# A second-level split for product 4 in the first superblock, and product 2's stored sums made one superblock later

## The chip, the cores and the metric

One core of one Trainium2 chip runs the kernel. The metric is device time in microseconds (us). Three runs of the kernel before took 1461.13, 1463.53 and 1457.79 us, so its median is 1461.13 us. One more execution was taken by the hardware profiler; all rows of the profile come from it, and their times count from the start of its span. TensorE, which multiplies, is called PE; VectorE is DVE, ScalarE is ACT, GpSimd is POOL, and SP is the queue of SyncE, which only starts transfers.

## The reference

```python
x: (8, 1024, 1024)   w1: (1024, 4096)   w2: (4096, 1024)   float32

h = x @ w1
h = 0.5 * h * (1 + np.tanh(np.sqrt(2 / np.pi) * (h + 0.044715 * h ** 3)))
return (h @ w2).astype(np.float32)
```

Two matrix products with a GELU between them. The kernel computes in fp16 with float32 accumulation.

## The kernel before

**Blocks and products.** The 8192 rows of x are worked off in eight superblocks of 1024 rows. In each, both matmuls are done by Winograd's form of Strassen's method: the operands are cut into 2 x 2 blocks ("11", "12", "21", "22"), sums and differences of blocks are formed, and seven products of half size take the place of eight. The products are numbered 1 to 7. Products 1, 2 and 3 use a weight block as it is, products 5, 6, 7 and 4 use sums of weight blocks (`SUMS` is 5, 6, 7, 4).

**Second level.** A product can be cut once more in the same way, which the class `Inner` does: seven small products of 16 matmuls on 256 columns each (L1129), in place of 64 matmuls on 512 columns (L1184). For that it needs the split of the weight operand: the four small sums 5, 6, 7 and 4 of it, which `split_jobs` makes, and the four small differences of the other operand, which `Inner.make` makes.

**Superblocks 0 and 1** are the first to see the weights. `matmul1` makes the first matmul in eight pairs of columns (j = 0 to 7), and `matmul2_made` the second. In them the sums of W2 are made (`make`, L890 stores them in superblock 1), and the splits of every W2 operand, too. The splits go to HBM, into `in_d[m]`, so that superblocks 2 to 7 (`matmul1_late`, `matmul2`) can run all seven products of the second matmul on the second level. Which products run on the second level in superblocks 0 and 1 is set by `deep`: product 3 in superblock 0, product 4 in superblock 1.

**The order around the change.** The second matmul of superblocks 0 and 1 runs its products in the order 1, 2, 5, 6, 3, 7, 4. A plain product has four steps, one for each 128 rows (q = 0 to 3); a product on the second level has seven (n = 1 to 7), in the order 1, 5, 6, 2, 7, 3, 4 of its small products. After each step, `run` works off the jobs that the table `FILL[sb]` has for it, written by hand. "36:p25" means: after step 6 of product 3, make small sum 5 of product 2's split. The letters are

- `g`: the sums of the GELU's output, which lie in pool "gcp" or over their operands;
- `w53`: piece 3 of W2's sum 5; sum 6 is made over block 11, sum 7 over block 12, sum 4 over block 21;
- `p25`: small sum 5 of product 2's split, with its store (L1012 from POOL's queue, L166 from SP's);
- `a45`: small difference 5 of product 4's other operand;
- `t`: the transposes of one block of the next x (SP's queue, in superblock 0);
- `x5`, `q5`, `i2`: sums of the next x, sums of W1's quad 0, and the small sums of one operand of the next first matmul.

DVE works these jobs off in program order, together with the additions that bring a product out of PSUM (`post`). In superblock 1 all sixteen transposes of the next x are issued together, in the program after step 0 of product 5.

**Queues.** `load_in_order` issues on SP's queue and keeps the program's order there. An entry whose data or buffer isn't ready holds up what stands behind it. `nc.gpsimd.dma_start` issues on POOL's queue. Before, product 2's and 3's splits are stored through SP, all others through POOL.

**Buffers.** Pool "up" has 24 buffers of 4 KB per partition (`unit`, `half`). In the second matmul of superblocks 0 and 1 the W2 pieces hold 16 of them (four for each block, or for the sum made over it), sum 5 another 4, the four blocks of the next x 4; the splits, W1's quad 0 for the next superblock and the result rows of a product on the second level want the rest. A store's buffer comes free when the store has landed. Pool "mp" has two buffers, which hold small sums 7 and 4.

**The first matmul of superblock 1** loads W1's quad 0 back (four loads issued through SP after step 0 of product 7), makes its sums 5, 6, 7, 4 on DVE and then, for the later superblocks, small sums of its operands 7 and 3 (pair j = 0) and 1 and 5 (pair j = 2), as `FIRST_INNER` says; those of operand 2 are `i2` in the table. Each is four additions of 128 x 512.

Of the kernel before, what the change touches and what calls it, by code (L numbers as in the profile page):

```python
# [9 lines left out]
DT = mybir.dt.float16  # L10
# [4 lines left out]
P = 128  # L15
# [8 lines left out]
SUMS = tuple(W_SUM)  # L24
# [13 lines left out]
""".split()  # L38
BEGIN = {"m37": (0,), "m24": (1,2), "m34": (3, 4)}
SPLIT_IN_M1 = ()  # L40
FIRST_INNER = {0: (7, 3), 2: (1, 5)}


def slots(table):
    return {(int(k[0]), int(k[1])): v.split() for k, v in (row.split(":") for row in table.split(";"))}
# [4 lines left out]
    ;20:g50 w50 w51;21:g51 w52;22:w53 g52;23:g53 p14  # L50
    ;50:w60 w61;51:w62 w63;52:g30 g31;53:g32 g33
    ;60:p35 p36 t0;61:a35 p37 t1;62:a37 p34 t2;63:t3 a36
    ;31:w70;32:a33;33:w71;34:w72;35:w73;36:p25;37:p26
    ;70:p27 p24;71:w40 w41;72:w42 w43;73:x5;40:x7;41:x6;42:x3 q5 q6 q7 q4
    ;43:i2""".replace("\n    ", "")),
    slots("""10:g60 w50;11:g61 w51;12:g62 w52;13:g63 w53
    ;20:g50 p55;21:g51 p56;22:g52 p57;23:g53 p54
    ;50:w60 w61;51:w62 w63;52:g30 g31;53:g32 g33
    ;60:p65 w70;61:p66 w71;62:p67 w72;63:p64 w73
    ;30:p75 w40;31:p76 w41;32:p77 w42;33:p74 w43  # L60
    ;70:p45 x5;71:p46 a45;72:x7 p47;73:a47 a46
    ;42:p44;43:a43;44:x6;45:x3;46:i2;47:i3""".replace("\n    ", "")),
)


# [11 lines left out]
def kernel(  # L77
# [7 lines left out]
    nc = tc.nc  # L85
# [10 lines left out]
    NI = I // P // 2  # L96
    OH = O // 2
# [10 lines left out]
    mp = ctx.enter_context(tc.tile_pool(name="mp", bufs=2))  # L108
# [15 lines left out]
    in_d = {m: dram.tile([P, 4, NI // 2, OH // 2], DT, name=f"in_d{m}") for m in range(1, 8)}  # L124
# [7 lines left out]
    def psum():  # L132
        return pp.tile([P, HT], F32, name="ps")
# [4 lines left out]
    def unit(rows, cols):  # L138
        return up.tile([P, rows, cols], DT, name="u")
# [396 lines left out]
    def matmul1(xs, sb, quads, start=None):  # L536
# [26 lines left out]
        for j in range(NI // 2):  # L563
# [60 lines left out]
            for job in jobs[:half]:  # L624
                job()
            for m in FIRST_INNER.get(j, ()) if sb == 1 else ():
                quads[0].inner_sums(m)
# [222 lines left out]
    def matmul2_made(sb, g, keep_w1, xb):  # L850
# [24 lines left out]
        def keep(b):  # L875
            if sb == 0:
                for q in range(NI // QC):
                    load_in_order(w2_at(q, term.get(b, b)), raw[b][q])
# [13 lines left out]
        def pieces(m):  # L892
            return raw[W_TERM[m]] if m in W_TERM else sums[m]

        def rows(t, q):
            return t[:, :, q * P:(q + 1) * P]

        s2, a, p5, t6, at = {}, {}, {}, {}, {}
        operands = {1: "11", 2: "12", 4: "22", 7: "21", 5: "11", 3: "12"}
        parts = {m: {} for m in (1, 2, 3, *SUMS)}  # L900
        splits = {m: split_jobs(m, lambda m=m: pieces(m), parts[m]) for m in parts}
        deep = {m: Inner(m, g[operands[m]]) for m in ((3,), (4,))[sb]}
        for m, d in deep.items():
            d.base, d.y = [], parts[m]
            d.rows = lambda r, t, o={3: "12", 4: "21"}[m], q=load_in_order if m == 3 else nc.gpsimd.dma_start: store_rows(sb, o, r, t, q)
# [1 line left out]
        def run(key):  # L907
            for job in FILL[sb].get(key, ()):
                kind, m, n = job[0], int(job[1]), int(job[2:] or 0)
                if kind == "g" and m == 6:  # L910
                    s2[n] = gcp.tile([P, NI, P], GT, name="gc")
                    tt(s2[n], rows(g["22"], n), rows(g["21"], n), SUB, True)
                elif kind == "g" and m == 5:
                    tt(rows(g["11"], n), s2[n], rows(g["11"], n), ADD, True)
                elif kind == "g":
                    tt(rows(g["12"], n), rows(g["12"], n), s2[n], SUB, True)
                elif kind == "w":
                    make(m, n)
                elif kind == "p":
                    splits[m][SUMS.index(n)]()  # L920
                elif kind == "a":
                    deep[m].make(n)
                elif kind == "t":
                    x_transpose(xb, load_in_order, xs.blocks, (m,))
                elif kind == "x":
                    xs.make(m, pin=True)
                elif kind == "q":
                    quad.sum(m, pin=True)
                elif kind == "i" and sb:
                    xs.make_inner(m)  # L930
                elif kind == "i":
                    quad.inner_sums(m)

        def post(m, q, bank):
            after = deep.get({6: 3, 7: 4}.get(m))
            if after:
                if q % 2 == 0:
                    after.base.append(half())
                so_far = after.base[q // 2][:, q % 2, :]
            if after and m == 6:  # L940
                tt(so_far, p5[q], bank, ADD, True)
            elif m in (1, 5, 6):
                t = {1: a, 5: p5, 6: t6}[m]
                t[q] = temp()
                act_copy(t[q], bank)
            elif m == 4:
                c = temp()
                act_copy(c, bank)
                store(sb, "21", q, c)
            else:  # L950
                t = {2: a, 3: t6, 7: p5}[m][q]
                tt(t, t, bank, ADD, True)
                at[q] = store(sb, {2: "11", 3: "12", 7: "22"}[m], q, t)
            if after and m == 7:
                act_copy(so_far, bank)
# [8 lines left out]
        for m, name, first in (  # L964
            (1, "a", True), (2, "b", True), (5, "c", True), (6, "a", False),
            (3, "c", False), (7, "a", False), (4, "a", False),
        ):
            if m in deep:
                deep[m].pieces = pieces(m)
                for n in deep[m].steps(deep[m].base):  # L970
                    if (m, n) == (4, 1):
                        quad = StoredHalf(0)
                    run((m, n))
                continue
            for q in range(NQ):
                if first:
                    banks[name].append(psum())
                bank = banks[name][q]
                matmuls2(bank, s2[q] if m == 6 else rows(g[operands[m]], q), pieces(m), first)
                post(m, q, bank)  # L980
                if (m, q) == (5, 0) and sb == 0:
                    xb = x_cast(sb + 1, nc.gpsimd.tensor_copy(out=pace, in_=p5[0][:, :2]))
                if (m, q) == (5, 3):
                    keep("22")
                if (m, q) == ((5, 0) if sb else (6, 0)):
                    xs = XOps(x_transpose(xb, load_in_order, which=range(4 if sb else 0)))
                if (m, q) == (7, 0) and sb == 0:
                    quad = MadeQuad(0, False, True)
                if (m, q) == (1, NQ - 1) and sb == 0:
                    sums[5] = [unit(2, HALF) for _ in range(NI // QC)]  # L990
                    for t in sums[5]:
                        act_copy(t[:, 0, :1], warm)
                    bring("22", act_copy, True)
                    keep("21")
                    keep("12")
                run((m, q))
        return xs, [quad]

    def split_jobs(m, pieces, t):

        def operand(v, h):
            if isinstance(v, int):
                return t[v][:, h * QC:(h + 1) * QC, :]
            k, b = int(v[0]) - 1, int(v[1]) - 1
            return chunks(pieces()[2 * k + h])[:, b]

        def make(n):
            u, op, v = W_SUM[n]
            t[n] = (mp.tile([P, NI // 2, OH // 2], DT, name="mu") if n in (7, 4) and m != 4 else unit(NI // 2, OH // 2))
            for h in range(2):  # L1010
                tt(t[n][:, h * QC:(h + 1) * QC, :], operand(u, h), operand(v, h), op, True)
            (load_in_order if m in (2, 3) else nc.gpsimd.dma_start)(out=in_d[m][:, SUMS.index(n)], in_=t[n])  # L1012

        return [lambda n=n: make(n) for n in SUMS]

# [166 lines left out]
    def matmuls2(bank, a, pieces, first):  # L1182
        for c in range(NI):
            tc.keep_in_program_order(nc.tensor.matmul(  # L1184
                pair(bank),
                lhsT=a[:, c, :],
                rhs=chunks(pieces[c // QC])[:, :, c % QC, :],
                start=(first and c == 0),
                stop=(c == NI - 1),
                skip_group_check=not first,  # L1190
            ))
# [93 lines left out]
    for sb in range(NSB):  # L1285
        if sb < 2:
            g, nxt = matmul1(xs, sb, quads, first if sb == 0 else None)
            xs, quads = matmul2_made(sb, g, None if sb else quads[-1].keep_raw, nxt)
            continue
        g, early, nxt = matmul1_late(xs, sb, quads, g_late or g_tiles())  # L1290
# [32 lines left out]
```

## Time and profile before

| | us |
|---|---|
| median of three runs | 1461.13 |
| lowest and highest of them | 1457.79, 1463.53 |
| the profiled execution's own time | 1460.05 |
| its span | 1458.30 |

| stage of the profiled execution | from, to (us) |
|---|---|
| superblock 0, first matmul | 0, 112.7 |
| superblock 0, products 1, 2, 5, 6 | 112.7, 168.0 |
| superblock 0, product 3 (second level) | 168.0, 180.2 |
| superblock 0, product 7, product 4 | 180.2, 194.1, 208.0 |
| superblock 1, first matmul | 209.3, 309.3 |
| superblock 1, products 1, 2, 5 | 309.3, 323.2, 337.0, 350.8 |
| superblock 1, products 6, 3, 7 | 350.8, 364.6, 378.4, 392.2 |
| superblock 1, product 4 (second level) | 392.2, 404.5 |
| superblocks 2 to 7, some 175 us each | 404.5, 1458.3 |

How to read the rows: a row of an engine's order of time gives the start, the duration, the engine and line, the operation, the tile written and read, the number of instructions merged into it, and in brackets the idle time ahead of it and what ended that. Rows of the stages give for each engine its busy time and its count, then the clock that TensorE was granted, the mean busy share of the 16 DMA engines, and what they moved. A row of the waits gives who waited for whom, the total, how often, and the longest. The granted clock is 1.00 in all stages. The page names L142 for nearly all of DVE's work, since one helper records it; which job a row is follows from its place in the tables and from its shape: two instructions of 128 x 1024 are one `p` job, one of 128 x 2048 is a `w`, `a`, `x` or `q` job.

### The profile page before, as it was taken

How to read it: one execution, taken by the hardware profiler on the slowest of the kernel's cores; microseconds unless marked ns; L12 is line 12 of the kernel's file. 1: busy time of each engine (PE TensorE's matmuls, PEld its weight loads, DVE VectorE, ACT ScalarE, POOL GpSimd, SP SyncE). 2: the span in 40 equal slices, each digit the busy share in tenths (PEclk: the TensorE clock that was granted, in tenths of full speed). 3: DMA queues.
4: the chain of work that ended last, by engine and by line, in shares of the span. 5: the costliest groups of instructions: out<-in, count | busy, mean ns of one | idle time of the engine just before them, and what ended most of it. 6: DMA issues, size and time to landing. Idle time of an engine off the chain costs nothing.

```text
span 1458.3 us, 28912 instructions
## 1 busy us (share of the span) xinstructions
PE 1447.5 (99%) x10731; PEld 1048.6 (72%) x10731; DVE 1210.6 (83%) x2019; ACT 711.6 (49%) x1460; POOL 583.1 (40%) x596
## 2 busy tenths in 40 slices
PE   9999999999999999999999999999999999999998
PEld 5444644444577888778877788777887778877887
DVE  5657859758788889888898898988989889888887
ACT  5665115641168621785128841488225872168621
POOL 1442113213369401792028820498005960068400
PEclk9999999999999999999999999999999999999999
DMA  9999999898799999999999999999999999986594
GB/s 329 339 334 381 320 279 368 303 302 260 276 387 249 289 373 367 340 231 337 356 359 311 240 364 347 365 283 234 384 352 364 253 265 371 358 338 230 203 409 168
DMA packets 199372, 460.13 MB, mean 316 GB/s; under 512 B 75200, under 2 KB 80320, under 8 KB 198336
## 3 DMA queue, kind: packets, MB, share of 16 engines
q1 hardware_dynamic: 179328, 378.59, 75.9%
q0 software_dynamic: 19904, 79.70, 17.1%
q8 instruction: 84, 1.38, 0.4%
q14 instruction: 56, 0.46, 0.1%
HBM read 370.15 MB, written 102.76 MB: 324 GB/s over the span
## 4 chain that ended last, share of the span: by engine, by line
PE 85%; DMA 8%; issue 4%; POOL 1%; DVE 1%; ACT 0%; SPq 0%; POOLq 0%; DVEq 0%
PE ps L1129 36%; PE ps L719 23%; PE ps L502 19%; PE ps L1184 6%; DMA gc<-in_w_dram 3%; DMA u<-in_w_dram 2%; DMA w_d<-u 1%; PE ps L435 1%; POOL u L172 1%; DMA xb<-in_x_dram 1%; DVE u L142 0%; PE ps L412 0%; SPq L166 0%; ACT u L169 0%; DMA u<-in_x_dram 0%
## 5 line engine op out<-in xcount | busy, mean ns | idle before, releaser
L169 ACT COPY tmp<-ps 128x512 f32<-128x512 f32 (+1 forms) x528 | 263.6, 539 | 231.1 <-PE ps L502 146.5
L502 PE MATMUL ps<-u 128*128 128x512 f16 x1472 | 343.8, 379 | 4.4 <-DVE tmp L142 1.9
L1129 PE MATMUL ps<-u,gc 128*128 128x256 f16 x2704 | 308.7, 273 | 0.0
L1129 PEld LDWEIGHTS <-gc 128*128 128x128 f16 x2816 | 275.5, 98 | 32.1 <-DMA u<-in_d 0.2
L142 DVE TENSOR_TENSOR tmp<-tmp,ps 128x256 f32<-128x256 f32 (+1 forms) x368 | 197.2, 544 | 72.7 <-PE ps L719 31.0
L142 DVE TENSOR_TENSOR u<-u 128x2048 f16<-128x2048 f16 (+3 forms) x292 | 223.4, 808 | 33.6 <-PE ps L1129 14.1
L502 PEld LDWEIGHTS <-u 128*128 128x128 f16 x1472 | 143.8, 98 | 146.8 <-issue 3.0
L719 PEld LDWEIGHTS <-u 128*128 128x128 f16 x2096 | 205.1, 98 | 57.2
L1129 PE MATMUL ps<-u,g 128*128 128x256 f16 x2000 | 234.8, 273 | 0.0
L848 POOL DMA_DIRECT2D out_dram<-u x48 | 35.2, 733 | 491.4 <-DVE u L142 433.4
L1129 PEld LDWEIGHTS <-g 128*128 128x128 f16 x2112 | 206.6, 98 | 24.4
L719 PE MATMUL ps<-u 128*128 128x256 f16 x1372 | 221.0, 273 | 0.0
L169 ACT COPY ps<-ps 128x256 f32<-128x256 f32 (+1 forms) x208 | 95.2, 458 | 219.3 <-PE ps L1129 219.3
L515 ACT ACTIVATE g<-tmp 128x512 f16<-128x512 f32 x282 | 173.9, 639 | 57.5 <-DVE tmp L142 56.6
L142 DVE TENSOR_TENSOR ps<-tmp,ps 128x256 f32<-128x256 f32 x444 | 181.3, 426 | 17.1 <-PE ps L719 9.4
L169 ACT COPY u<-ps 128x512 f32<-128x512 f32 (+1 forms) x114 | 66.3, 587 | 179.9 <-PE ps L1129 146.2
L142 DVE TENSOR_TENSOR u<-u,ps 128x512 f32<-128x512 f32 x174 | 118.4, 684 | 40.1 <-PE ps L1129 19.3
L515 ACT ACTIVATE g<-ps 128x512 f16<-128x512 f32 x230 | 137.9, 600 | 25.3 <-PE ps L719 15.3
L1184 PE MATMUL ps<-u,g 128*128 128x512 f16 x640 | 138.8, 379 | 0.0
L771 POOL TENSOR_TENSOR tmp<-tmp 128x512 f32<-128x512 f32 x96 | 122.0, 1273 | 40.6 <-DVE tmp L142 30.5
L142 DVE TENSOR_TENSOR tmp<-ps,tmp 128x512 f32<-128x512 f32 x126 | 86.7, 690 | 49.0 <-PE ps L502 41.6
L1184 PEld LDWEIGHTS <-g 128*128 128x128 f16 x640 | 62.6, 98 | 75.3
(72 smaller groups left out, 1570.7 us busy)
## 6 DMA issues: line engine op xcount, KB each, us to landing
u<-w_d SPq DMA_DIRECT2D x347, 512.0 KB, 9.3
u<-in_d SPq DMA_DIRECT2D x162, 512.0 KB, 9.7
gc<-in_w_dram SPq DMA_DIRECT2D x48, 512.0 KB, 5.9
out_dram<-u POOLq DMA_DIRECT2D x48, 512.0 KB, 7.4
g<-w_d SPq DMA_DIRECT2D x45, 512.0 KB, 8.2
w_d<-u POOLq DMA_DIRECT2D x40, 512.0 KB, 6.8
w_d<-u SPq DMA_DIRECT2D x32, 512.0 KB, 10.0
xb<-in_x_dram POOLq DMA_DIRECT2D x56, 256.0 KB, 6.9
```

What stands on the lines that cost most here:

```text
L142: i = nc.vector.tensor_tensor(out=out, in0=in0, in1=in1, op=op)
L169: tc.keep_in_program_order(nc.scalar.copy(out=out, in_=in_))
L172: pool_last[0] = nc.gpsimd.tensor_copy(out=out, in_=in_)
L435: tc.keep_in_program_order(nc.tensor.matmul(bank[:, cols], lhsT=w[:, k, :], rhs=self.xs.blocks[f"{a}{r}"][:, k, cols], start=r == 1 and k ...
L502: tc.keep_in_program_order(nc.tensor.matmul(bank, lhsT=w, rhs=x, start=first and k == 0, stop=k == n - 1, skip_group_check=not first,))
L515: gelu_last[0] = nc.scalar.activation(out=out, in_=src, func=GELU, scale=scale)
L719: tc.keep_in_program_order(nc.tensor.matmul(out, lhsT=w, rhs=x, start=first and k == 0, stop=k == 1, skip_group_check=not first,))
L771: tc.keep_in_program_order(nc.gpsimd.tensor_tensor(out=t, in0=t, in1=temp("p", m), op=ADD))
L848: return start(out=rows, in_=src)
L1129: tc.keep_in_program_order(nc.tensor.matmul(bank[:, i * OH // 2:(i + 1) * OH // 2], lhsT=t[:, c, i * P:(i + 1) * P], rhs=self.weights(j, c ...
L1184: tc.keep_in_program_order(nc.tensor.matmul(pair(bank), lhsT=a[:, c, :], rhs=chunks(pieces[c // QC])[:, :, c % QC, :], start=(first and c ...
```

## The change

Four things are changed.

1. In superblock 0 product 4 runs on the second level too (`deep` has 3 and 4). Its split is made there from sum 4, and not stored (`keep` is false): superblock 1 makes and stores it, as before. w40 to w43 are made earlier, since the split needs all of sum 4; x5, x7, x6, x3 and the sums of W1's quad 0 move into the steps of product 4.
2. Product 2's split (p25, p26, p27, p24) is made and stored in superblock 1, in the steps of product 6, instead of superblock 0. All four of its small sums take buffers of pool "up".
3. The splits of products 5 and 6 in superblock 1 are stored through SP's queue instead of POOL's, as is product 2's.
4. Operand 2's small sums of W1's quad 0 move from the table into pair 0 of superblock 1's first matmul; operand 3's go to pair 2, operand 1's to pair 4, operand 5's to pair 6. In superblock 1, x5 and x7 are made some steps later.

```diff
-FIRST_INNER = {0: (7, 3), 2: (1, 5)}
+FIRST_INNER = {0: (2, 7), 2: (3,), 4: (1,), 6: (5,)}
...
 FILL = (
...
-    ;31:w70;32:a33;33:w71;34:w72;35:w73;36:p25;37:p26
-    ;70:p27 p24;71:w40 w41;72:w42 w43;73:x5;40:x7;41:x6;42:x3 q5 q6 q7 q4
-    ;43:i2
+    ;31:w70;32:a33;33:w71;34:w72;35:w73;36:w40;37:w41 w42
+    ;70:w43 p45;71:p46 a45;72:p47 a47;73:a46;41:p44;42:a43;43:x5;44:x7;46:x6;47:q5 x3 q6 q7 q4
...
-    ;60:p65 w70;61:p66 w71;62:p67 w72;63:p64 w73
+    ;60:p65 w70 p25;61:p66 w71 p26;62:p67 w72 p27;63:p64 w73 p24
     ;30:p75 w40;31:p76 w41;32:p77 w42;33:p74 w43
-    ;70:p45 x5;71:p46 a45;72:x7 p47;73:a47 a46
-    ;42:p44;43:a43;44:x6;45:x3;46:i2;47:i3
+    ;70:p45;71:p46 a45;72:p47 a47;73:a46 x5
+    ;42:p44;43:a43 x7;44:x6;45:x3;46:i2;47:i3
...
-        splits = {m: split_jobs(m, lambda m=m: pieces(m), parts[m]) for m in parts}
-        deep = {m: Inner(m, g[operands[m]]) for m in ((3,), (4,))[sb]}
+        splits = {m: split_jobs(m, lambda m=m: pieces(m), parts[m], sb or m != 4) for m in parts}
+        deep = {m: Inner(m, g[operands[m]]) for m in ((3, 4), (4,))[sb]}
...
-                    if (m, n) == (4, 1):
+                    if (m, n) == (4, 1) and sb:
                         quad = StoredHalf(0)
...
-    def split_jobs(m, pieces, t):
+    def split_jobs(m, pieces, t, keep=True):
...
-            t[n] = (mp.tile([P, NI // 2, OH // 2], DT, name="mu") if n in (7, 4) and m != 4 else unit(NI // 2, OH // 2))
+            t[n] = (mp.tile([P, NI // 2, OH // 2], DT, name="mu") if n in (7, 4) and (m not in (2, 4) or not keep) else unit(NI // 2, OH // 2))
...
-            (load_in_order if m in (2, 3) else nc.gpsimd.dma_start)(out=in_d[m][:, SUMS.index(n)], in_=t[n])
+            if keep:
+                (load_in_order if m in (2, 3, 5, 6) else nc.gpsimd.dma_start)(out=in_d[m][:, SUMS.index(n)], in_=t[n])
```

More of the change, by code (lines that the diff above doesn't have):

```diff
@@ L52 @@
     ;60:p35 p36 t0;61:a35 p37 t1;62:a37 p34 t2;63:t3 a36
-    ;31:w70;32:a33;33:w71;34:w72;35:w73;36:p25;37:p26
-    ;70:p27 p24;71:w40 w41;72:w42 w43;73:x5;40:x7;41:x6;42:x3 q5 q6 q7 q4
-    ;43:i2""".replace("\n    ", "")),
+    ;31:w70;32:a33;33:w71;34:w72;35:w73;36:w40;37:w41 w42
+    ;70:w43 p45;71:p46 a45;72:p47 a47;73:a46;41:p44;42:a43;43:x5;44:x7;46:x6;47:q5 x3 q6 q7 q4""".replace("\n    ", "")),
     slots("""10:g60 w50;11:g61 w51;12:g62 w52;13:g63 w53
@@ L58 @@
     ;50:w60 w61;51:w62 w63;52:g30 g31;53:g32 g33
-    ;60:p65 w70;61:p66 w71;62:p67 w72;63:p64 w73
+    ;60:p65 w70 p25;61:p66 w71 p26;62:p67 w72 p27;63:p64 w73 p24
     ;30:p75 w40;31:p76 w41;32:p77 w42;33:p74 w43
-    ;70:p45 x5;71:p46 a45;72:x7 p47;73:a47 a46
-    ;42:p44;43:a43;44:x6;45:x3;46:i2;47:i3""".replace("\n    ", "")),
+    ;70:p45;71:p46 a45;72:p47 a47;73:a46 x5
+    ;42:p44;43:a43 x7;44:x6;45:x3;46:i2;47:i3""".replace("\n    ", "")),
 )
```

## The prediction, made before the changed kernel was run

> **What bounds the kernel now.** I read the profile's page first, then busy time by stage, then TensorE's (PE's) own order of work, and last the two queues that the change moves work between: VectorE (DVE) and SyncE's DMA queue (SP).
>
> ```profile
> span 1458.3 us, 28912 instructions
> PE 1447.5 (99%) x10731; PEld 1048.6 (72%) x10731; DVE 1210.6 (83%) x2019; ACT 711.6 (49%) x1460; POOL 583.1 (40%) x596
> ```
>
> PE has some 11 us of gaps in 1458. A change can gain by less PE work or by closing gaps, and lose by opening new ones. Which gaps lie near the change is shown by PE's order of time around the end of superblock 0 (start, duration, what ended the idle time ahead):
>
> ```profile
> 199.63 8.37 PE L1184 MATMUL ps<-u,g 128*128 128x512 f16 x38
> 209.31 3.63 PE L502 MATMUL ps<-u 128*128 128x512 f16 x16 [1.32 <-DMA u<-w_d]
> 213.54 8.81 PE L502 MATMUL ps<-u 128*128 128x512 f16 x40 [0.60 <-DVE u L142]
> 223.29 24.69 PE L502 MATMUL ps<-u 128*128 128x512 f16 x112 [0.95 <-DVE tmp L142]
> 248.91 7.28 PE L502 MATMUL ps<-u 128*128 128x512 f16 x33 [0.93 <-DVE tmp L142]
> ```
>
> Four gaps, 1.32 + 0.60 + 0.95 + 0.93 = 3.80 us, all just after superblock 0: the first waits for quad 0 of W1 to be loaded back, the others for DVE. From 248.91 on the chain of waits is PE alone; its rows for the second matmul of superblock 1 also price both kinds of product:
>
> ```profile
> 309.50 82.88 PE ps L1184 x384
> 392.38 12.23 PE ps L1129 x112
> ```
>
> A plain product is 64 of the first kind, 64 x 82.88/384 = 13.81 us; a product on the second level is 12.23 us. Last, the stages (busy us and count, clock, DMA share, GB/s):
>
> ```profile
> core 0: us, PE busy (x) PEld busy (x) DVE busy (x) ACT busy (x) POOL busy (x), PEclk, DMA share, GB/s
> 180.20:194.10 13.90, 13.90 (x67) 6.32 (x65) 9.54 (x15) 0.00 (x0) 1.14 (x2) 1.00 0.80 179
> 194.10:208.00 13.90, 13.90 (x65) 6.09 (x63) 7.82 (x8) 1.76 (x3) 1.62 (x3) 1.00 0.98 296
> 350.80:364.60 13.80, 13.80 (x66) 6.26 (x65) 7.91 (x10) 2.35 (x4) 4.61 (x8) 1.00 0.77 289
> 364.60:378.40 13.80, 13.80 (x65) 6.27 (x64) 9.08 (x12) 0.59 (x1) 4.30 (x8) 1.00 0.34 132
> ```
>
> These are products 7 and 4 of superblock 0 and products 6 and 3 of superblock 1. DVE has 4 to 6 us of slack in each, and DMA is idle two thirds of the last.
>
> **The change, part by part.**
>
> *Product 4 of superblock 0.* 64 matmuls go, 112 of half width come: 12.23 - 13.81 = **-1.58 us** of PE. DVE gets four differences (a45, a46, a47, a43) and six additions into the sums. The nearest rows:
>
> ```profile
> 165.39 1.22 DVE L142 TENSOR_TENSOR gc<-g 128x2048 f16<-128x2048 f16 x1
> 183.93 0.69 DVE L142 TENSOR_TENSOR tmp<-tmp,ps 128x512 f32<-128x512 f32 x1 [0.80 <-PE ps L1184]
> 184.53 1.29 DVE L142 TENSOR_TENSOR mu<-u 128x1024 f16<-128x1024 f16 x2
> 189.39 1.29 DVE L142 TENSOR_TENSOR mu<-u 128x1024 f16<-128x1024 f16 x2 [3.57 <-DMA in_d<-mu]
> ```
>
> That is 4 x 1.22 + 6 x 0.69 = 9.0 us, against the 27.8 - 17.36 = 10.4 us idle in the two stages; product 4's splits replace product 2's at the same 1.29 each. w40 to w43 come earlier, into the end of product 3. By position each operand is ready before PE asks (a45 is done at about 190, its use is at 195.9; a46 at 196, its use at 197.6), so I cost it at nothing. Without that cover the price is the excess, at most one job per step, some 1 to 2 us. Four copies by ACT and four quarter-megabyte stores become two half-megabyte ones: nothing.
>
> *Product 2's stores leave superblock 0.* The SP queue there:
>
> ```profile
> 185.99 11.86 SPq L166 DMA_TRANSPOSE u<-xb  x8
> 198.58 0.46 SPq L166 DMA_DIRECT2D in_d<-u  x1
> 199.12 1.07 SPq L166 DMA_DIRECT2D out_dram<-u  x1
> 200.31 1.17 SPq L166 DMA_DIRECT2D in_d<-u  x1
> 201.59 4.12 SPq L166 DMA_DIRECT2D u<-w_d  x4
> ```
>
> The four quad loads, whose lateness is the gap of 1.32, stand behind two of product 2's stores. These go: 0.46 + 1.17 = 1.63 us of the queue, and 2 x 0.52 MB ahead in the engines, 3.5 us at the 296 GB/s of that stage. I take loads 2.6 us earlier, midway. Both bounds: 0 earlier, if the transposes decide alone, and all 3.80 us of gaps closed. With 2.6, the first load lands at 206.7, PE is ready at 208.0 - 1.58 = 206.4: gap 0.3 in place of 1.32. DVE's part:
>
> ```profile
> 201.51 5.00 DVE L142 TENSOR_TENSOR u<-u 128x2048 f16<-128x2048 f16 x4 [4.50 <-DMA out_dram<-u]
> 212.26 4.79 DVE L142 TENSOR_TENSOR u<-u 128x2048 f16<-128x2048 f16 x4 [5.74 <-DMA u<-w_d]
> 236.74 4.48 DVE L142 TENSOR_TENSOR u<-u 128x512 f16<-128x512 f16 x12
> 246.70 1.56 DVE L142 TENSOR_TENSOR u<-u 128x512 f16<-128x512 f16 x4 [2.22 <-DMA w_d<-u]
> 270.76 0.69 DVE L142 TENSOR_TENSOR tmp<-ps,tmp 128x512 f32<-128x512 f32 x1 [4.61 <-PE ps L502]
> ```
>
> q5 starts when the loads have landed (212.26, then 209.7), so the gap of 0.60 stays; x3 now stands between q5 and q6 (1.2 us), so product 6 waits about 0.5. Ahead of the first product 7 the small sums fall from 12 to 8 (i2 comes, i3 and the old i2 go), 4 x 0.37 = 1.5 us, about 0.4 more than x3 costs: 0.95 becomes 0.55. At the third pair the small sums halve, and the wait of 2.22 for a buffer, just ahead of the gap of 0.93, should go with them: 0. The two sets moved to pairs 4 and 6 (1.5 us each) meet idle DVE, as the 4.61 us at 270.76 for the first. Left: 0.3 + 0.6 + 0.5 + 0.55 = 1.95, so **-1.85 us**.
>
> *Product 2's splits and the stores of 5 and 6 in superblock 1.* This is where it can lose. The SP queue and the DVE of that stage before:
>
> ```profile
> 315.45 5.47 SPq L166 DMA_TRANSPOSE u<-xb  x4
> 319.39 7.11 SPq L166 DMA_TRANSPOSE u<-xb  x5
> 334.47 5.75 SPq L166 DMA_TRANSPOSE u<-xb  x4
> 338.43 8.24 SPq L166 DMA_TRANSPOSE u<-xb  x5
> SPq L166 <- DMA in_d<-u: 7.8, 1, 7.8
> 338.98 1.29 DVE L142 TENSOR_TENSOR mu<-u 128x1024 f16<-128x1024 f16 x2
> 357.49 1.22 DVE L142 TENSOR_TENSOR u<-u 128x2048 f16<-128x2048 f16 x1
> 368.32 0.69 DVE L142 TENSOR_TENSOR tmp<-tmp,ps 128x512 f32<-128x512 f32 x1 [9.61 <-PE ps L1184]
> ```
>
> The 7.8 us wait says that the third x block took the buffer of p55: pool "up", 24 buffers, was full (16 weight pieces, 4 of sum 5, two x blocks, p55, p56). Product 5's stores now stand on SP ahead of the transposes, so the 16 transposes start after p54 (338.98 + 1.29 = 340.3), not at 315. Product 6's and product 2's stores queue behind them. In product 6's stage only the four pieces of sum 5 come free; p65, p25, p66, p26 take them, and p27 has to wait until p65's store has landed. Behind p27 on DVE stand p64, w73 (product 7 needs it at 378.4), p24 and all of product 3's additions. Pace of the transposes: 1.44 us each (5.75/4) gives their end at 340.9 + 23.0 = 363.9. A store's landing:
>
> ```profile
> DMA to landing us min/median/max: 3.0/6.2/10.3
> 394.28 1.23 DVE L142 TENSOR_TENSOR gc<-g,gc 128x2048 f16<-128x2048 f16 x1
> 393.97 3.66 PE L1129 MATMUL ps<-u,gc 128*128 128x256 f16 x32
> ```
>
> With the median, p27 starts at 363.9 + 0.5 + 6.2 = 370.6; w73 is done 3.5 us later, at 374.1, in time; the DVE queue reaches product 3's first addition at 375.3 instead of 368.3, 7.0 us late, of which the 9.61 us idle there had been the cover. It wins back 0.5 us in each step of 3.45 us, six times, and 1.65 in the step that x5 leaves: 2.4 us late at a46 (394.2 to 396.6), which PE wants at 393.97 + 3.66/2 = 395.8: **+0.8 us**. Bounds: with 1.23 us a transpose (11.05 us for nine) and 3.0 us landing the lag is 0.5 and costs nothing; the other end is rival A. Two of product 5's stores and all of 6's also leave the POOL queue, which has slack (4.6 of 13.8): nothing. The 2 MB extra fit into the stage where DMA is 0.34 busy.
>
> The Trainium skill, "DMA: Bandwidth & Descriptors", section "Issuing engines are not separate DMA queues", says that the engine which issues a DMA only saves issue time, since all run on the same 16 engines. By that rule the move to SP would be free. The waits just quoted speak against it here: an SP entry that waits holds everything behind it.
>
> **Sum.** -1.58 - 1.85 + 0.8 = -2.6 us. The profiled execution took 1460.05 us (span 1458.3 plus 1.75 around it), so 1457.4 in its terms; the median of the three runs shown is 1461.13, 1.1 us above it, with a spread from 1457.79 to 1463.53. For a median I forecast 1461.13 - 2.6 = **1458.5 us**, no change that a measurement tells (0.5% is 7.3 us).
>
> **Rivals.**
>
> *A, the queue behind the transposes costs more than DVE's idle time.* They compete with POOL's stores in a stage of DMA share 0.77, and in superblock 0 they have been slower:
>
> ```profile
> 170.25 8.73 SPq L166 DMA_TRANSPOSE u<-xb  x4
> ```
>
> At 8.73/4 = 2.18 us each they end at 375.8, p65 lands 10.8 later at 386.6, w73 is done at 390.1: PE waits 11.7 us at product 7, and DVE's lag of then some 11 us, less 4.6 won back, costs about 5 more at a46. With -3.4 that is +13: 1474 us. It decides from the point where p65 lands later than 374.9 (378.4 - 3.5). For it: the one full pool. Against: the rows of superblock 1 itself show 1.2 to 1.4 us each. I give 0.15, most of it between +3 and +13.
>
> *B, the quad loads come no earlier.* If the transposes and their DMA work alone set when the loads land, PE reaches the same wait 1.58 us earlier and waits that much longer; only the gap of 0.93 goes, and the 0.8 is paid: 1461.0 us. For it: the transposes are the last entry in both orders. Against: the two stores stand between. 0.20.
>
> *C, the queue's place is free.* If the pool has one buffer more than I count, or p65 lands by 364, there is no lag: -3.4, 1457.7 us. That is also what the skill's rule above would give. Against: the 7.8 us wait on a buffer. 0.15.
>
> **How the numbers follow.** The forecast itself (1455.5 to 1461) has 0.50. Below 1453.8 (faster by over 0.5%) would need all 3.80 us of gaps closed, no lag and a fast draw of runs: 1461.13 - 1.58 - 3.80 = 1455.75, so 0.04. Slower by over 0.5% (above 1468.4) is the upper part of A, 0.11. The rest, 0.85, is within. The range is from 1455.75 less 2 us of spread between runs up to the lower half of A: 1453.5 to 1466. The likeliest case's own range lies inside.
>
> **What would show it.** Right: product 4 of superblock 0 on L1129 in about 12.2 us; the quad loads issued near 199.5 and PE's gap ahead of the first L502 of superblock 1 under 1 us; transposes in superblock 1 starting near 337 to 341 in one run of 21 to 23 us; a DVE wait ended by the landing of in_d in product 6's stage, and PE's gap at a46 below 2 us. Wrong: a gap of PE ahead of product 7 (rival A), quad loads still issued after 201 (B), no DVE wait on in_d in that stage (C), or the loads of superblock 2's first weights late at 404, since they queue on SP behind all this.

## The result and the profile after

The changed kernel took 1455.95 us (median of 8 runs, 1455.37 to 1457.97), the kernel before, beside it on the same chip, 1461.12 us (8 runs, 1457.79 to 1463.58). The ratio is 0.9966 with a 95% interval of 0.9954 to 0.9978: 5.2 us less. That is under the 0.5% which the prediction calls no change, but the interval lies clear of 1. The forecast was 1458.5 us, 2.6 us less, so the direction was right and the gain about twice as large as forecast. The changed kernel's runs also scatter less: over 2.6 us, where those of before scatter over 5.8.

The profiled execution of the changed kernel took 1457.25 us. PE's order of time in it, from the end of superblock 0 to the start of superblock 2 (L501 is the first matmul, which was L502 before; L1184 and L1129 are the plain and the second-level products, as before):

```profile
168.97 1.91 PE L1129 MATMUL ps<-u,g 128*128 128x256 f16 x16
...
181.19 13.98 PE L1184 MATMUL ps<-u,g 128*128 128x512 f16 x64
195.01 1.91 PE L1129 MATMUL ps<-u,g 128*128 128x256 f16 x16
...
205.49 1.91 PE L1129 MATMUL ps<-mu,g 128*128 128x256 f16 x16
207.24 96.97 PE L501 MATMUL ps<-u 128*128 128x512 f16 x448
304.04 41.60 PE L1184 MATMUL ps<-u,g 128*128 128x512 f16 x192
...
399.15 2.75 PE L501 MATMUL ps<-u 128*128 128x512 f16 x12
401.74 0.60 PE L718 MATMUL ps<-u 128*128 128x256 f16 x4
403.19 3.63 PE L501 MATMUL ps<-u 128*128 128x512 f16 x16 [0.85 <-DMA u<-w_d]
```

Product 4 of superblock 0 now takes 207.24 - 195.01 = 12.23 us. The first matmul of superblock 1 is one row of 448 matmuls: all four gaps are gone. A new one of 0.85 us stands at 403.19, for weights of superblock 2. The rows of before that answer to these, the start of product 3 of superblock 0 and the start of superblock 1's second matmul:

```profile
167.98 1.91 PE L1129 MATMUL ps<-u,g 128*128 128x256 f16 x16
...
309.34 1.03 PE L1184 MATMUL ps<-u,g 128*128 128x512 f16 x4
```

The account between the two executions: product 3 of superblock 0 started 0.99 us later, superblock 1's second matmul 5.30 us earlier. So 6.29 us were won between them, 1.58 by PE's work and 4.71 by gaps. (Their rows said 3.80: a PE row ends with its last matmul's modelled end, some 0.15 us after PE could have gone on, and waits too short to break a row are not listed.) Behind 399 us some is lost again. From the start of superblock 2 to the start of PE's last sixteen matmuls it is 1049.35 us (399.15 to 1448.50), where it was 1048.08 before (404.45 to 1452.53), and the last store ended 1.2 us later in relation to PE's end; the span is 2.8 us shorter. The second profile of the same kernel, below, won 6.40 us between the start of product 3 and superblock 1's second matmul (167.90 to 302.86). It has no listed gap at 403, but short waits at 426 to 428 and at 499, and takes 1049.44 us from the start of superblock 2. That the two spans of before and after differ by nearly the 2.6 us of the forecast is chance, then: a larger gain, a later start of product 3 and losses that nobody forecast add up to it.

The SP queue of the changed kernel, in both places that the prediction spoke of:

```profile
185.87 11.26 SPq L165 DMA_TRANSPOSE u<-xb  x8
197.23 1.07 SPq L165 DMA_DIRECT2D out_dram<-u  x2
198.40 3.60 SPq L165 DMA_DIRECT2D u<-w_d  x4
...
331.54 3.77 SPq L165 DMA_DIRECT2D in_d<-mu  x2
335.53 23.18 SPq L165 DMA_TRANSPOSE u<-xb  x16
358.81 3.16 SPq L165 DMA_DIRECT2D in_d<-u  x4
```

The four quad loads are issued at 198.40, not 201.59. The transposes of superblock 1 start behind product 5's stores and take 23.18 us in one run, and four stores of products 6 and 2 leave directly behind them. VectorE's order of time shows both ends:

```profile
208.04 5.76 DVE L141 TENSOR_TENSOR u<-u 128x2048 f16<-128x2048 f16 x5
...
241.40 1.55 DVE L141 TENSOR_TENSOR u<-u 128x512 f16<-128x512 f16 x4 [3.09 <-DMA w_d<-u]
...
343.96 7.18 DVE L141 TENSOR_TENSOR u<-u 128x1024 f16<-128x1024 f16 x10
351.05 1.29 DVE L141 TENSOR_TENSOR mu<-u 128x1024 f16<-128x1024 f16 x2
352.25 1.22 DVE L141 TENSOR_TENSOR u<-u 128x2048 f16<-128x2048 f16 x1
361.82 1.29 DVE L141 TENSOR_TENSOR u<-u 128x1024 f16<-128x1024 f16 x2 [8.35 <-DMA in_d<-u]
363.03 1.29 DVE L141 TENSOR_TENSOR mu<-u 128x1024 f16<-128x1024 f16 x2
364.24 2.43 DVE L141 TENSOR_TENSOR u<-u 128x2048 f16<-128x2048 f16 x3
366.57 0.69 DVE L141 TENSOR_TENSOR tmp<-tmp,ps 128x512 f32<-128x512 f32 x1
...
387.73 1.22 DVE L141 TENSOR_TENSOR gc<-g,gc 128x2048 f16<-128x2048 f16 x1
```

q5, x3, q6, q7 and q4 run in one row at 208.04 with no wait ahead: the loads have landed. At 361.82 stands p27, after 8.35 us of waiting for the landing of a store (p65's), as the prediction had it. It starts only 3.0 us after that store was issued. w73 is the first of the three instructions of the row at 364.24, so it is done near 365.5, and a46 (387.73) is early enough: no gap of PE.

### The profile page after: what moved, and what is told of

It is laid out like the page before. It is cut to its first block, busy times and chain, and to the rows that moved or that the text cites. A ratio compares the mean times of both kernels' runs of the same rounds, so it can differ in the third digit from the quotient of the medians.

```text
span 1455.5 us, 29022 instructions
## 1 busy us (share of the span) xinstructions
PE 1445.7 (99%) x10779; PEld 1053.0 (72%) x10779; DVE 1223.2 (84%) x2037; ACT 712.5 (49%) x1462; POOL 580.5 (40%) x586
## 4 chain that ended last, share of the span: by engine, by line
PE 96%; DMA 2%; DVE 1%; SPq 0%; issue 0%; ACT 0%; DVEq 0%
PE ps L1129 37%; PE ps L501 25%; PE ps L718 23%; PE ps L1184 10%; DMA u<-w_d 1%; PE ps L434 1%; DMA gc<-in_w_dram 1%; DMA u<-in_d 0%; DVE u L141 0%; SPq L165 0%; SPq L288 0%; DVE tmp L141 0%; PE ps L411 0%; ACT u L230 0%; DVE ps L141 0%
## 5 line engine op out<-in xcount | busy, mean ns | idle before, releaser
L501 PE MATMUL ps<-u 128*128 128x512 f16 x1472 | 343.1, 379 | 1.2 <-DMA u<-w_d 0.9
L1129 PE MATMUL ps<-u,gc 128*128 128x256 f16 x2752 | 314.4, 273 | 0.2 <-DMA u<-in_d 0.2
L1129 PEld LDWEIGHTS <-gc 128*128 128x128 f16 x2880 | 281.6, 98 | 33.2 <-DVE gc L141 0.5
L141 DVE TENSOR_TENSOR u<-u 128x512 f32<-128x512 f32 (+3 forms) x300 | 228.2, 805 | 31.2 <-PE ps L1129 14.1
L501 PEld LDWEIGHTS <-u 128*128 128x128 f16 x1472 | 143.9, 98 | 142.6 <-DMA u<-w_d 1.1
L1129 PE MATMUL ps<-u,g 128*128 128x256 f16 x2032 | 238.7, 273 | 0.0
L1129 PEld LDWEIGHTS <-g 128*128 128x128 f16 x2160 | 211.4, 98 | 25.1
L141 DVE TENSOR_TENSOR u<-u,ps 128x512 f32<-128x512 f32 x180 | 122.6, 684 | 40.5 <-ACT u L168 20.0
L1184 PE MATMUL ps<-u,g 128*128 128x512 f16 x576 | 125.0, 379 | 0.0
L1184 PEld LDWEIGHTS <-g 128*128 128x128 f16 x576 | 56.3, 98 | 67.8
```

Of the source, the lines that this page charges most:

```text
L141: i = nc.vector.tensor_tensor(out=out, in0=in0, in1=in1, op=op)
L501: tc.keep_in_program_order(nc.tensor.matmul(bank, lhsT=w, rhs=x, start=first and k == 0, stop=k == n - 1, skip_group_check=not first,))
L1129: tc.keep_in_program_order(nc.tensor.matmul(bank[:, i * OH // 2:(i + 1) * OH // 2], lhsT=t[:, c, i * P:(i + 1) * P], rhs=self.weights(j, c ...
L1184: tc.keep_in_program_order(nc.tensor.matmul(pair(bank), lhsT=a[:, c, :], rhs=chunks(pieces[c // QC])[:, :, c % QC, :], start=(first and c ...
```

## The experiments

All were run beside the kernel before, on three chips, on which its medians were 1460.73, 1460.23 and 1460.12 us. Times are medians, and ratios are to the kernel before on the same chip.

### What closed the gaps

**move_only**: the kernel before, with product 2's splits in superblock 1 and the stores of products 2, 5 and 6 as changed; product 4 plain, small sums as before. Shown is superblock 0's part of the edit; superblock 1's rows of `FILL` and `split_jobs` are those of the changed kernel.

```diff
...
-    ;31:w70;32:a33;33:w71;34:w72;35:w73;36:p25;37:p26
-    ;70:p27 p24;71:w40 w41;72:w42 w43;73:x5;40:x7;41:x6;42:x3 q5 q6 q7 q4
+    ;31:w70;32:a33;33:w71;34:w72;35:w73
+    ;71:w40 w41;72:w42 w43;73:x5;40:x7;41:x6;42:x3 q5 q6 q7 q4
...
```

> The kernel before with one part of the change: product 2's splits and the stores of products 2, 5 and 6 as in the changed kernel; product 4 of superblock 0 stays plain, the small sums of W1's quad 0 stay where they were. Theory 1 (the quad loads were late because product 2's two stores stood ahead of them on SP): the first quad load is issued near 198.5 to 199.5, not 201.6, PE's gaps around 209 to 249 (1.32 + 0.60 + 0.95 + 0.93 in the rows) shrink to under 1 us in all, and the time is 1461 - 3 to 4 + about 1 for the new waits at 404 = 1458 to 1459 us. Theory 2 (the gaps closed because product 4's second level and the moved small sums set buffers and DVE free): at most the first gap shrinks, two or more us of gaps stay, 1460 to 1462 us.

It took 1457.71 us, ratio 0.9980 (0.9969 to 0.9991). PE in its profile:

```profile
207.77 96.86 PE L502 MATMUL ps<-u 128*128 128x512 f16 x448
```

No gap is left in that stage, with the quad loads issued at 198.75; the gap at 403 is there too (0.67). That is theory 1, with a time 0.3 us below its range. But the edit also takes four of VectorE's jobs out of these stages, so by itself it doesn't tell the stores' place in the queue from VectorE's load. The next run does.

**before_p2_pool**: the kernel before, with product 2's stores on POOL's queue.

```diff
-            (load_in_order if m in (2, 3) else nc.gpsimd.dma_start)(...)
+            (load_in_order if m in (3,) else nc.gpsimd.dma_start)(...)
```

> The kernel before with one word changed: product 2's stores in superblock 0 go through POOL's queue in place of SP's, so the same bytes move but no longer stand ahead of the quad loads. Theory 1a (it is the place in SP's queue): quad loads issued at 198.5 to 200, first gap under 0.7 us, 1458.5 to 1460 us. Theory 1b (it is the 2 MB in a stage where the DMA engines are full): loads issued early but landing no earlier than 208.5, first gap 1 us or more, 1460.5 to 1462 us.

1459.60 us, ratio 0.9992 (0.9982 to 1.0003): the times don't tell it from no change. The profile (an execution of 1457.54 us) has the loads issued at 198.86 and PE going on at 208.79 for 168 matmuls without a gap; it also has a new gap of 0.71 at 196.44 and one of 0.37 at 245.69. The 168 matmuls take in the places of the first three gaps, and for these it is theory 1a, the place in the queue.

**inner_only**: the kernel before, with the small sums of W1's quad 0 spread.

```diff
-FIRST_INNER = {0: (7, 3), 2: (1, 5)}
+FIRST_INNER = {0: (2, 7), 2: (3,), 4: (1,), 6: (5,)}
...
-    ;43:i2
```

> The kernel before with only the small sums of W1's quad 0 spread as in the changed kernel (operands 2 and 7 in pair 0, 3 in pair 2, 1 in pair 4, 5 in pair 6). Theory 1: the gap of 1.32 and that of 0.60 stay, that of 0.93 at 248.91 goes and that of 0.95 shrinks by about half, 1459.5 to 1460.5 us. Theory 2 (all four gaps follow from the late loads alone): all four stay within 0.3 us, 1460.5 to 1462 us.

1457.42 us, ratio 0.9980 (0.9964 to 0.9995): 3.3 us, more than either theory gave. Its profile has one gap of 0.41 at 211.19 and none at 223 or 249. In that execution SP was some 3 us ahead (loads issued at 198.71, though still behind the two stores), so the absence of the first gap may be the draw, and the early loads may have a share in that of the two later ones as well; the next run tests the sums from the other side. Spreading the sums and moving the stores each win about 3 us, but both, with PE's 1.58, win 5. That fits one lateness of VectorE on which both work.

**old_inner**: the changed kernel, with the small sums bunched again.

```diff
-FIRST_INNER = {0: (2, 7), 2: (3,), 4: (1,), 6: (5,)}
+FIRST_INNER = {0: (2, 7, 3), 2: (1, 5)}
```

> The changed kernel, with the small sums of W1's quad 0 bunched again as before (operands 2, 7 and 3 in pair 0, 1 and 5 in pair 2). Theory 1 (with the quad loads early, DVE has the room for them): gaps under 1 us in all, 1456 to 1457.2 us. Theory 2 (the bunched sums are the cause of the later gaps by themselves): 0.95 and 0.93 return, 1457.8 to 1459 us.

1457.86 us, ratio 0.9984 (0.9975 to 0.9992), 1.9 us over the changed kernel's median, and PE's rows say where:

```profile
218.58 24.33 PE L501 MATMUL ps<-u 128*128 128x512 f16 x112 [0.56 <-DVE tmp L141]
244.03 60.59 PE L501 MATMUL ps<-u 128*128 128x512 f16 x280 [1.12 <-DVE tmp L141]
```

The loads were issued at 196.91, early, and still the two later gaps are back, at the same two places as before (0.95 and 0.93 there). That is theory 2: in the changed kernel bunched sums make the later two gaps by themselves.

### What product 4 is worth, and what it needs

**plain4**: the changed kernel with product 4 of superblock 0 plain. **after_again**: the changed kernel beside it.

```diff
-        deep = {m: Inner(m, g[operands[m]]) for m in ((3, 4), (4,))[sb]}
+        deep = {m: Inner(m, g[operands[m]]) for m in ((3,), (4,))[sb]}
...
-    ;31:w70;32:a33;33:w71;34:w72;35:w73;36:w40;37:w41 w42
-    ;70:w43 p45;71:p46 a45;72:p47 a47;73:a46;41:p44;42:a43;43:x5;44:x7;46:x6;47:q5 x3 q6 q7 q4
+    ;31:w70;32:a33;33:w71;34:w72;35:w73
+    ;71:w40 w41;72:w42 w43;73:x5;40:x7;41:x6;42:x3 q5 q6 q7 q4
```

> The changed kernel with product 4 of superblock 0 plain again; product 2's splits, the queues and the spread small sums stay changed. Theory 1 (the second level is worth its matmuls, 13.81 - 12.23 = 1.58 us, and the gaps are closed by the other parts): no gap of PE over 0.5 us between 150 and 310 us, 1.2 to 2.0 us above the changed kernel, 1457.2 to 1458 us. Theory 2 (its jobs are also what sets DVE free after superblock 0): gaps return there, 1458.5 to 1460 us.

> The changed kernel once more, beside the other three on the same chip: 1455 to 1457 us, the gap at 403 between 0.5 and 1.2 us. A gap that is not there in this execution would mean that it is a matter of the draw.

plain4 took 1457.26 us, ratio 0.9975 (0.9965 to 0.9986), the changed kernel 1455.38 us, ratio 0.9959 (0.9944 to 0.9973): 1.9 us apart. In plain4 the first matmul of superblock 1 is one row of 448 matmuls from 207.75, with no gap. From the start of product 3 of superblock 0 to superblock 1's second matmul plain4 takes 136.55 us (167.89 to 304.44), the changed kernel beside it 134.96: 1.59 us, the price of the matmuls. That is theory 1. In this second profile of the changed kernel no gap at 403 is listed, so that gap is a matter of the draw; the largest waits that PE has in the whole run are:

```profile
PE ps L369 <- DVE warm L1280: 1.2, 1, 1.2
PE ps L411 <- DVE tmp L403: 0.7, 1, 0.7
PE ps L434 <- ACT u L168: 0.5, 1, 0.5
PE ps L1129 <- DMA u<-in_d: 0.2, 1, 0.2
PE ps L501 <- ACT tmp L168: 0.2, 1, 0.2
```

The first three are at the start of the run, the last two are the waits at 499 and 426.

**extra_stores** was to put the lateness of the quad loads back: two more 512 KB stores ahead of them on SP. **both_back** has the bunched sums as well.

```diff
                     run((m, n))
+                    if (sb, m, n) == (0, 3, 7):
+                        for j in (5, 6):
+                            load_in_order(in_d[3][:, SUMS.index(j)], parts[3][j])
```

> The changed kernel, with two more 512 KB stores on SP's queue between the transposes and the quad loads of superblock 0 (the small sums 5 and 6 of product 3's split, stored a second time to the same place), where product 2's two stores stood before. Theory 1 (late quad loads make gaps only where DVE is also behind, so the spread small sums alone hold most of the gain): quad loads issued near 201, a first gap of 0.5 to 1.5 us, the later ones under 0.3, 1456.5 to 1457.5 us against about 1456. Theory 2 (the place of the loads is the whole cause): the gaps return in full, 1459.5 to 1461 us.

> The changed kernel with both put back, the two extra stores ahead of the quad loads and the bunched small sums. Theory 1 (each of the two alone closes most of the gaps, only both together bring them): 3 to 4.7 us more than the changed kernel, 1459 to 1461 us, and clearly more than the sum of what each costs alone. Theory 2 (the two add): the sum of the two losses.

1467.64 us, ratio 1.0049 (1.0036 to 1.0063), and 1468.90 us, ratio 1.0057 (1.0041 to 1.0073): far outside all that was expected. The first's VectorE and PE:

```profile
186.69 0.69 DVE L141 TENSOR_TENSOR tmp<-tmp,ps 128x512 f32<-128x512 f32 x1 [0.25 <-PE ps L1187]
200.35 1.29 DVE L141 TENSOR_TENSOR u<-u 128x1024 f16<-128x1024 f16 x2 [12.98 <-DMA out_dram<-u]
```

```profile
202.84 3.59 PE L1132 MATMUL ps<-u,gc 128*128 128x256 f16 x16 [7.54 <-DVE gc L141]
207.51 3.51 PE L1132 MATMUL ps<-u,gc 128*128 128x256 f16 x16 [1.08 <-DVE gc L141]
```

And the stage behind the long gap, with the granted clock third from the end:

```profile
202.84:206.00 3.16, 3.16 (x15) 2.24 (x16) 3.16 (x5) 0.59 (x1) 0.54 (x1) 0.50 0.93 216
```

The edit did more than it was meant to: the stored tiles keep two buffers of pool "up" until the transposes ahead of them have been issued, so p46 waits 12.98 us for a buffer, and a45, a46 and PE behind it. The two gaps are 8.6 us. Another 3.3 us come from the clock: TensorE was granted 0.50 of it behind the long gap, and twice sixteen matmuls took 3.59 and 3.51 us, where they take 1.91. The question of the late loads is not answered by either run. They suggest why product 2's splits and product 4's second level don't go together in superblock 0: two more buffers held there by stores behind the transposes cost 11.7 us (1467.64 against 1455.95, on another chip), where the second level wins 1.58.

### The queue in superblock 1

**p5_pool** and **p56_pool**: the changed kernel, with the stores of product 5, or of products 5 and 6, back on POOL's queue.

```diff
-                (load_in_order if m in (2, 3, 5, 6) else nc.gpsimd.dma_start)(...)
+                (load_in_order if m in (2, 3, 6) else nc.gpsimd.dma_start)(...)      # p5_pool
+                (load_in_order if m in (2, 3) else nc.gpsimd.dma_start)(...)         # p56_pool
```

> The changed kernel, with product 5's stores back on POOL's queue; those of products 2 and 6 stay on SP's behind the transposes. Theory 1 (product 5's stores on SP hold the transposes up, these hold product 6's stores up, and the full pool turns that into DVE's wait of 8.35 us and the late weight loads of superblock 2): the transposes start near 310 and end by 342, DVE's wait on a landing store in product 6's stage is under 1 us, the gap of 0.85 at 403 goes, 1454.5 to 1455.5 us against about 1456 of the changed kernel. Theory 2 (the gap at 403 comes from the 2 MB of product 2's stores moved into superblock 1): the gap stays, 1455.5 to 1456.5 us.

> The changed kernel with the stores of products 5 and 6 both back on POOL's queue; product 2's stay behind the transposes. Theory 1 (stores on POOL's queue beside the transposes make these slow, 2.6 us each in the middle and 56 us in all where only product 5's stood there): the sixteen transposes take over 35 us again, and single times scatter over more than 5 us. Theory 2 (that profile was one slow execution): they take 20 to 32 us as in the kernel before, DVE's wait in product 6's stage goes since p65 no longer stands behind them, and the times lie within 3 us around 1455 to 1456.5.

p5_pool took 1456.29 us over twelve runs, ratio 0.9977 (0.9965 to 0.9990), with three of them above 1460; the profiled one, 1462.85, was the slowest, so its profile shows the kernel at its worst. p56_pool took 1462.25 us, ratio 1.0006 (0.9985 to 1.0027): the whole gain is gone. Its twelve runs lie between 1453.92 and 1469.42; the fastest is below every run of the changed kernel, so what makes it slow is not there each time. The transposes in p56_pool (count, shortest, median and longest issue in ns, first and last start; then the landings):

```profile
L165 SPq DMA_TRANSPOSE u<-xb x16: 1362/2696/9088, 307.8 to 365.1; - x16
...
DMA to landing us min/median/max: 6.4/16.5/24.4
```

and in the changed kernel:

```profile
L165 SPq DMA_TRANSPOSE u<-xb x16: 1193/1263/2347, 335.5 to 357.5; - x16
...
DMA to landing us min/median/max: 2.9/4.4/8.8
```

They start 28 us earlier and end 9 later. What the DMA engines did meanwhile, p56_pool first (the stage, then clock, DMA share, GB/s):

```profile
320.00:340.00 20.00, 1.00 1.17 190
340.00:360.00 20.00, 1.00 1.20 204
```

```profile
320.00:340.00 20.00, 1.00 0.56 192
340.00:360.00 20.00, 1.00 0.98 213
```

The two second rows are the ones to compare, since the changed kernel's transposes only start at 335.5: with transposes under way the engines' share is 1.20 for 204 GB/s in p56_pool and 0.98 for 213 GB/s in the changed kernel. VectorE in p56_pool then waits 10.68 and 8.38 us for landings, and PE 5.16 us at a46:

```profile
392.64 3.59 PE L1129 MATMUL ps<-u,gc 128*128 128x256 f16 x16 [5.16 <-DVE gc L141]
```

The sixteen matmuls behind this gap take 3.59 us instead of 1.91, at a granted clock of 0.50, so the gap costs 1.7 us more than its length.

In all eight profiles in which product 5's stores stand ahead of all sixteen transposes on SP, these start some 31 us into that matmul and take 22.5 to 23.8 us. Where product 5's stores are on POOL, the transposes start at 307.8 to 315.4 and take 31.2 (before), 30.7 (before_p2_pool), 34.6 (inner_only), 56.2 (p5_pool) and 59.7 us (p56_pool). But POOL's stores alone don't make them slow. This is the kernel before:

```profile
L166 SPq DMA_TRANSPOSE u<-xb x16: 1157/1284/1792, 315.4 to 345.0; - x16
```

Its median issue of 1.28 us is that of the changed kernel, and 7.8 us of its 31.2 are the wait for a buffer that the prediction read; before_p2_pool has 1.31 us and a wait of 7.9. Among these five profiles an earlier start goes with slower transposes: 1.28 us (start at 315.4), 1.31 (311.9), 1.51 (311.0), 2.59 (308.3), 2.70 (307.8). So the numbers of theory 1 of p56_pool came, 59.7 us and a scatter of 15.5 us, but its cause, POOL's stores beside the transposes, is not shown. In p5_pool the expectation that an early start means an early end fell: in its profile they end at 364.5, and VectorE waits 15.13 us for a landing.

**split_t**: the transposes in two halves, the second behind the stores of products 6 and 2.

```diff
-                    xs = XOps(x_transpose(xb, load_in_order, which=range(4 if sb else 0)))
+                    blocks = x_transpose(xb, load_in_order, {b: unit(KH, HT) for b in ("22", "21")}, range(2))
...
+                if (m, q) == (6, 3) and sb:
+                    blocks.update({b: unit(KH, HT) for b in ("12", "11")})
+                    xs = XOps(x_transpose(xb, load_in_order, blocks, range(2, 4)))
```

> The changed kernel, with the sixteen transposes of superblock 1 in two halves: those of blocks 22 and 21 after step 0 of product 5 as now, those of blocks 12 and 11 after step 3 of product 6, behind the stores of products 6 and 2; their two buffers of pool up are claimed only then. Theory 1 (p27 waits for a buffer that a store behind sixteen transposes holds; that lag makes the weight loads of superblock 2 late): DVE's wait of 8.35 us on a landing store in product 6's stage goes, the gap of 0.85 at 403 and the one of 0.2 to 0.4 at 490 go, 1454.5 to 1455.3 us. Theory 2 (the gap at 403 is a matter of DMA bytes): the wait goes and the gap stays, 1455.7 to 1456.5 us.

1457.05 us, ratio 0.9977 (0.9965 to 0.9990), one run of twelve at 1463.58. VectorE's wait is gone, PE's at 403 is not:

```profile
363.36 0.69 DVE L141 TENSOR_TENSOR tmp<-tmp,ps 128x512 f32<-128x512 f32 x1 [4.80 <-PE ps L1190]
```

```profile
403.59 3.63 PE L501 MATMUL ps<-u 128*128 128x512 f16 x16 [0.91 <-DMA u<-w_d]
```

That is theory 2, with a time some 0.5 us above its range: p27's wait lay inside VectorE's idle time and cost nothing, so taking it away wins nothing. The second half of the transposes then took 15.70 us, against 12.74 for the first: it had POOL's stores of product 7 beside it.

**pin_loads**: the weight loads of superblock 2's first three halves in the program's order.

```diff
-                        quad = StoredHalf(0)
+                        quad = StoredHalf(0, load=load_in_order)
...
-                quads += [StoredHalf(i) for i in range(len(quads), min(j + 3, n))]
+                quads += [StoredHalf(i, load=load_in_order if sb == 2 and j == 0 else nc.sync.dma_start)
+                          for i in range(len(quads), min(j + 3, n))]
```

> The changed kernel, with the weight loads of superblock 2's first three halves in the program's order on SP's queue, so that the five loads of half 0 go ahead of the two loads into pool mp, which stand at the head of that queue until 381 to 385 waiting for small sums 7 and 4 of product 7 to land. Theory 1 (the gap at 403 is half 0's loads landing late behind 1 MB that is needed later): the gap goes, 0.5 to 1.3 us less than the changed kernel, 1454.7 to 1455.5 us. Theory 2 (the loads wait for buffers or the engines are full whatever the order): the gap stays, same time.

1456.20 us, ratio 0.9965 (0.9951 to 0.9978), beside 1455.38 of the changed kernel. The gap at 403 is absent in its profile, but it isn't listed in the changed kernel's second one either, and the times show no gain. So neither theory is borne out in full: the gap can be gone and nothing is won. None of the versions tried is shown to be faster than the changed kernel.

## Why the prediction was right, point by point

- **Product 4, -1.58 us.** Right: 12.23 us in the trace, and 1.59 us between the profiles of plain4 and the changed kernel. That the jobs are covered was right, too, in both profiles of the changed kernel; x5 waited 0.42 and 0.50 us for a buffer, no more. The cover is thin, though. In the profiles of split_t and pin_loads, whose edits don't touch superblock 0, x5 waited 2.28 and 2.12 us, and PE 0.82 and 0.66 us in product 4.
- **Quad loads earlier.** Right in mechanism and near in size: issued 3.2 us earlier (2.6 taken). From the end of the transposes to the first load it was 3.74 us before (197.85 to 201.59) and is 1.27 us now (197.13 to 198.40), so 2.5 us are the queue's place; the rest is the transposes' earlier end in this execution.
- **Gaps, -1.85 us.** This is the term that was mis-sized: 4.71 us were won. The step "Left: 0.3 + 0.6 + 0.5 + 0.55 = 1.95" kept four remainders, and the rows of the changed kernel list none of them in either profile. It took the lateness of each gap for itself, while they follow a late VectorE: q5 started 2.95 us after PE's first matmul of that stage before (212.26 against 209.31) and starts 0.80 us after it now (208.04 against 207.24), and what the other gaps wait for stands behind q5 in VectorE's order. The bunched sums add to that lateness, as old_inner shows. The wait of 2.22 us for a buffer, which was to go, stayed (3.09 us at 241.40), without a listed gap behind it. And the step read the gaps at 3.80 from rows that leave out their edges.
- **p27's wait in superblock 1, +0.8 us.** The chain was right link by link (start behind p54, a full pool, p27 blocked, 8.35 us). The cost was not. The landing took 3.0 us, the shortest in the rows of before, where the median of 6.2 was taken (the working also goes from 340.3 to 340.9 for the start of the transposes without naming a term). VectorE reached product 3's first addition at 366.57; in the kernel before it was 368.32, which is 363.02 with the 5.30 us by which the stage now starts earlier. So it came 3.5 us late, not 7.0, and had made that up by a46. split_t shows that the wait costs nothing.
- **"Leave the POOL queue ... nothing."** Not so in the changed kernel: with the stores of products 5 and 6 left on POOL, p56_pool takes 6.9 us more in the median (1462.25 against 1455.38), and its times scatter over 15 us. The prediction counted the transposes' later start as a risk; in the profiles it goes with transposes that are done in 23 us.
- **Rival A** (transposes at 2.18 us each) did not happen in the changed kernel. It did in p5_pool's and p56_pool's profiles (2.6 and 2.7 us), with the gap at a46 that it named (5.16 us in p56_pool), but with none ahead of product 7. **Rival B** fell with the loads at 198.40. **Rival C** came true in its price, though not in its sign: p65 had landed by 361.8, ahead of the 364 that it named, and nothing was paid, but VectorE did wait for it. The Trainium skill's rule in "DMA: Bandwidth & Descriptors", section "Issuing engines are not separate DMA queues", that the issuing engine only saves issue time, is no guide to the whole time here. In p56_pool the same bytes go through another queue, the transposes start 28 us earlier, and the kernel takes 6.9 us more.
- **The loads at 404**, named as a sign of being wrong, were 0.85 us late in one profile of the changed kernel and nearly in time in the other.

Still open: what in the engines makes the early transposes slow. POOL's stores alone are ruled out, since the kernel before has them beside transposes of 1.28 us; no run varied the start of the transposes by itself. Open, too, is why the last store ends 1.2 us later in relation to PE's end. How much the late quad loads alone cost in the changed kernel wasn't measured either, since extra_stores measured buffers instead.

## What to carry to other kernels

A queue entry that waits for its data can be worth having: it holds back what stands behind it, and a transfer started early into full engines may end later than one started late. Before a store is moved behind others, count the buffers that it then holds; a pool with too few buffers can cost an engine's whole wait, and TensorE a lower clock behind it. And gaps in a row that come from one late engine go together, so price the lateness once.

## What the runs showed of the hardware

Sixteen transposes by DMA took very different times: in p56_pool 2.70 us each in place of the changed kernel's 1.26 us (median), landing after 16.5 us in place of 4.4, with the DMA engines' share at 1.17 to 1.20 while they moved 190 to 204 GB/s. The changed kernel moved 213 GB/s at a share of 0.98 during its transposes, and 385 GB/s at a share of 1.01 in the stage behind them:

```profile
360.00:380.00 20.00, 1.00 1.01 385
```

The granted clock of TensorE fell behind long gaps: to 0.50 behind 7.54 us in extra_stores and 5.16 us in p56_pool, and to 0.57 behind 2.75 us in p5_pool (393.75 to 397.2). Behind the gap of 1.32 us in the kernel before it stayed at 1.00.
